# Delta rule: the part that needs the roots of keys and queries, issued three projection steps later

## The chip, the core and the metric

The kernel runs on one core of a Trainium2 chip. The metric is the device time of one execution in microseconds. The engines are TensorE (PE in the rows; PEld is its weight load), VectorE (DVE), ScalarE (ACT), GpSimd (POOL) and SyncE (SP), which issues the DMAs here.

## The reference

A two-layer decoder trunk on a sequence of 2048 rows of 1024: a gated DeltaNet layer, then a forgetting-attention layer. Only the first is touched. Cut to what matters:

```python
qkv = silu(causal_depthwise_conv(qkv, conv_w))      # 4 taps
q, k, v = split(qkv, 3)
q, k = l2_norm(q), l2_norm(k)                       # per head, 128 channels, 8 heads
...
a_mat = where(strict, einsum('cd,sd->cs', k * beta, k) * decay, 0)
attn  = einsum('cd,sd->cs', q, k) * decay
u, w  = triangular_solve(I + a_mat, [v * beta, k * beta * exp(gcum)])
...                                                 # per chunk: state S from u, w, k, attn
```

The root is that of `l2_norm`: `rsqrt(sum(x*x) + eps)` for each row of q and k.

## The kernel before

The first stage walks over four blocks of 512 rows (q0 to q3) and in each over four pairs of heads, so over 16 pairs. For one pair `project` issues eight projections in the order K, Q, V of the first head, K, Q, V of the second, then the gates z of both. A projection is eight steps (`kt` 0 to 7) of three 128x128x512 matmuls (L130 to L132), with a `yield` after each step. Weights come through SP (L312, L313) for blocks after the first; in q0 they are split on ScalarE and POOL on the way (L320, L322).

Behind each of K, Q and V stands a `tail`: ScalarE makes two copies of the product (L386, L390), VectorE adds the three other taps of the convolution (L387, three L392), ScalarE takes a tanh (L395), and VectorE makes the SiLU of it (L400), into `kq` for keys and queries. `tail` returns a `rest`, which goes into the list `pend`; it is taken out at step 6 of a later projection, when more than one stands there. So the `rest` of Q runs at step 6 of the projection after next: of the second head's K for the first head, of the first gate z for the second. It transposes on TensorE (L407), takes squares on ScalarE (L411), adds eps on VectorE (L417), and POOL takes the power -0.5 (`rsqrt`, L119). Then come what needs the root: four small instructions on VectorE (L419 to L424, which give `rq`, `brk2` and `vs`), and per two chunks the products of keys with keys and queries on TensorE (L430) and three wide instructions on VectorE (L434 twice, L437), which write `At` and `attn`.

Beside the projections of one pair runs `finish` of the pair before, a generator that `weave` advances after every step. It reads `At`: four DMAs out (L469), four back in another shape (L472), a substitution of 62 dependent VectorE instructions (L478, L480), DMAs back (L483, L485), then transposes into `Tn` (L488). After 45 steps it goes on with the solver's products on TensorE (L494, into X1 by L498 and L499, then L505), and after these with the recurrence over the chunks (L540 to L577), whose results are scaled (L595) and written out (L599, L601).

A scheduler places the instructions of each engine in a list before the run: among those that it expects to be ready, the one that comes first in the program goes first, and one from further down may fill a hole. Each engine then works through its list in order. Tiles come from pools with a few buffers each; the product tile `pk` and the decay's `pdf` share two PSUM buffers.

Of the kernel before, what the change touches and what calls it, by code (L numbers as in the profile page):

```python
# [9 lines left out]
F32 = mybir.dt.float32  # L10
# [4 lines left out]
ALU = mybir.AluOpType  # L15
# [3 lines left out]
P = 128  # L19
# [5 lines left out]
SCALE = P ** -0.5  # L25
# [103 lines left out]
def mm3(nc, out, ah, al, bh, bl, start, stop):  # L129
    nc.tensor.matmul(out, ah, bh, start=start, stop=False)  # L130
    nc.tensor.matmul(out, ah, bl, start=False, stop=False)  # L131
    nc.tensor.matmul(out, al, bh, start=False, stop=stop)  # L132


def gdn(k, ins, oT_d, chain, proj_, after_proj):

    nc, tc = k.nc, k.tc
    NQ, TB, CH = 4, 512, 4
# [12 lines left out]
    pq = pool(proj_, "gpq", 2, "right", space=PSUM)  # L151
# [143 lines left out]
    def project(qt, hg, state, tiles):  # L295
        xh, xl = state[:2]
        q_ = f"q{qt}"
        gn = f"{q_}g{hg}"
        kqs, vRs, kds, late = [], [], [], []
        At = c2.tile([P, U, P], F32, tag="At", name=f"At_{gn}")  # L300
        attn = c2.tile([P, U, P], F32, tag="attn", name=f"attn_{gn}")
        zT = c2.tile([P, G, TB], F32, tag="zT", name=f"zT_{gn}")
        rq = c2.tile([P, U], F32, tag="rq", name=f"rq_{gn}")
# [24 lines left out]
        def proj(col, nm):  # L328
            wh, wl = wsplit(col, nm)
            pp = pm.tile([P, TB], F32, tag="mm", name=f"pp_{nm}")  # L330
            if turns:
                turns.pop(0)()
            for kt in range(KT):
                if len(turns) > 1:
                    turns.pop(0)()
                mm3(nc, pp, wh[:, kt, :], wl[:, kt, :], xh[kt], xl[kt], kt == 0, kt == KT - 1)
                if kt == 6 and len(pend) > 1:
                    pend.pop(0)()
                yield
            if turns:  # L340
                turns.pop(0)()
            return pp
# [15 lines left out]
        for hl in range(G):  # L358
            h = hg * G + hl
            us = slice(hl * CH, (hl + 1) * CH)  # L360
            kq = c2.tile([P, CH, 2, P], F32, tag="kq", bufs=4, name=f"kq_{q_}_{h}")
            vR = c2.tile([P, CH, P], F32, tag="vR", bufs=4, name=f"vR_{q_}_{h}")
            kd = c2.tile([P, CH, P], F32, tag="kd", bufs=4, name=f"kd_{q_}_{h}")
            kqs.append(kq)
            vRs.append(vR)
            kds.append(kd)
            E = p2.tile([P, CH, P], F32, tag="E", name=f"E_{q_}_{h}")
            if len(state) > 2:
                decays(h, E)
            else:  # L370
                late.append(lambda: decays(0, E))
            ssn = p2.tile([P, 2, CH], F32, tag="ssn", name=f"ssn_{q_}_{h}")
            rn = p2.tile([P, 2, CH], F32, tag="rn", name=f"rn_{q_}_{h}")
            vs = p2.tile([P, CH], F32, tag="vs", name=f"vs_{q_}_{h}")
            for kind in (1, 0, 2):
                ct = kind * H + h
                nm = f"{q_}_{ct}"
                pp = yield from proj(ct * P, nm)
                if len(late) > 0:
                    late.pop(0)()  # L380
                beta, eg = state[2], state[5]

                def tail(h=h, hl=hl, us=us, kq=kq, vR=vR, kd=kd, E=E, ssn=ssn, rn=rn, vs=vs, kind=kind, ct=ct, nm=nm, pp=pp):
                    cx = p2.tile([P, TB + 3], F32, tag="cx", name=f"cx_{nm}")
                    nc.vector.tensor_copy(cx[:, 0:3], halo[:, ct, :])
                    nc.scalar.copy(cx[:, 3:], pp)  # L386
                    nc.vector.tensor_copy(halo[:, ct, :], cx[:, TB:TB + 3])  # L387
                    cw = [k.cols[:, C_CONV + j * 24 + ct:C_CONV + j * 24 + ct + 1] for j in range(4)]
                    acc = p2.tile([P, TB], F32, tag="acc", name=f"acc_{nm}")
                    nc.scalar.activation(acc, pp, AF.Copy, scale=cw[3])  # L390
                    for j in range(3):
                        nc.vector.scalar_tensor_tensor(out=acc, in0=cx[:, j:j + TB], scalar=cw[j], in1=acc,  # L392
                                                       op0=ALU.mult, op1=ALU.add)
                    th = p2.tile([P, TB], F32, tag="th", bufs=3, name=f"th_{nm}")
                    nc.scalar.activation(th, acc, AF.Tanh, scale=0.5)  # L395
                    if kind == 2:
                        src = th.rearrange("p (c t) -> p c t", t=P)
                    else:
                        src = kq[:, :, 1 - kind, :]
                    nc.vector.scalar_tensor_tensor(out=src, in0=th.rearrange("p (c t) -> p c t", t=P), scalar=1.0,  # L400
                                                   in1=acc.rearrange("p (c t) -> p c t", t=P),
                                                   op0=ALU.add, op1=ALU.mult)

                    def rest():
                        pt = pm.tile([P, CH, P], F32, tag="tr", name=f"pt_{nm}")
                        for c in range(CH):
                            nc.tensor.transpose(out=pt[:, c, :], in_=src[:, c, :], identity=k.ident)  # L407
                        if kind < 2:
                            for c in range(CH):
                                junk = p2.tile([P, P], BF16, tag="junk2", name=f"j_{nm}_{c}")  # L410
                                nc.scalar.activation(junk, pt[:, c, :], AF.Square, accum_out=ssn[:, kind, c:c + 1])  # L411
                        if kind == 1:
                            for c in range(CH):
                                nc.scalar.activation(kd[:, c, :], pt[:, c, :], AF.Copy,
                                                     scale=eg[:, 2, c, h:h + 1])
                        if kind == 0:
                            nc.vector.tensor_scalar(out=ssn, in0=ssn, scalar1=4.0 * EPS, scalar2=None, op0=ALU.add)  # L417
                            rsqrt(k, rn.rearrange("p a b -> p (a b)"), ssn.rearrange("p a b -> p (a b)"), 2 * CH)
                            nc.vector.tensor_scalar(out=rq[:, us], in0=rn[:, 0], scalar1=SCALE, scalar2=None,  # L419
                                                    op0=ALU.mult)  # L420
                            nc.vector.tensor_tensor(out=brk2[:, us], in0=rn[:, 1], in1=rn[:, 1], op=ALU.mult)
                            nc.vector.tensor_tensor(out=brk2[:, us], in0=brk2[:, us], in1=beta[:, :, h],
                                                    op=ALU.mult)
                            nc.vector.scalar_tensor_tensor(out=vs, in0=ssn[:, 1], scalar=0.5, in1=rn[:, 1],  # L424
                                                           op0=ALU.mult, op1=ALU.mult)
                            for cc in range(0, CH, 2):
                                pk = pq.tile([P, 2, 2, P], F32, tag="kkq", name=f"pk_{q_}_{h}_{cc}")
                                for c in (cc, cc + 1):
                                    u = hl * CH + c
                                    nc.tensor.matmul(pk[:, c - cc].rearrange("p a b -> p (a b)"), kq[:, c, 0, :],  # L430
                                                     kq[:, c].rearrange("p a b -> p (a b)"), start=True, stop=True)
                                for c in (cc, cc + 1):
                                    u = hl * CH + c
                                    nc.vector.scalar_tensor_tensor(out=At[:, u, :], in0=pk[:, c - cc, 0, :],  # L434
                                                                   scalar=brk2[:, u:u + 1], in1=E[:, c, :],
                                                                   op0=ALU.mult, op1=ALU.mult)
                                nc.vector.tensor_tensor(out=attn[:, hl * CH + cc:hl * CH + cc + 2, :], in0=pk[:, :, 1, :],  # L437
                                                        in1=E[:, cc:cc + 2, :], op=ALU.mult)
                        if kind == 2:
                            for c in range(CH):  # L440
                                nc.scalar.activation(vR[:, c, :], pt[:, c, :], AF.Copy, scale=vs[:, c:c + 1])

                    return rest

                pend.append(tail())


        for hl in range(G):
            h = hg * G + hl
# [150 lines left out]
                                           in1=zT[:, hl, :], op0=ALU.mult, op1=ALU.mult)  # L600
            nc.sync.dma_start(oT_d[h, :, t0:t0 + TB], og)  # L601

    pend = []
    state = prep(0)
    sides = []
    for qt in range(NQ):
# [704 lines left out]
```

## Time and profile before

| | us |
|---|---|
| median of three runs | 2905.1 (2903.18 to 2905.47) |
| profiled execution | 2906.06 |
| its span | 2904.3 |
| TensorE busy | 2797.7 (96%) |
| VectorE busy | 1715.9 (59%) |
| ScalarE busy | 1335.7 (46%) |
| POOL busy | 704.6 (24%) |

Busy time is the time in which the engine had an instruction in work; ends of matmuls are modelled. Times in rows are counted from the start of the span. In a row of the timeline the first number is the start, the second the time that the instructions of the row took together, `x4` their count, and the bracket the engine's idle time just before and who ended it.

### The profile page before, as it was taken

To read this page: it belongs to the slowest core of one execution; us is meant where nothing else is said; L and a number is where in the kernel's file an instruction comes from. 1 tells how busy PE (TensorE), PEld (TensorE's weight loads), DVE (VectorE), ACT (ScalarE), POOL (GpSimd) and SP (SyncE) were. 2 spreads that over 40 slices of the span, in tenths; PEclk is the share of its full clock that TensorE was granted. 3 is DMA by queue.
4 is the path that set the end of the run, shared out by engine and by line. 5 is a ranking of instruction groups with operands and counts; after the bars stand their busy time and mean duration, and the time that the engine had idled before them with its cause. 6 is when DMAs were issued, how large, how long until landed. Compare 5 with 4: busy or idle time off the path is not lost.

```text
span 2904.3 us, 50700 instructions
## 1 busy us (share of the span) xinstructions
PE 2797.7 (96%) x18406; PEld 2434.2 (84%) x18406; DVE 1715.9 (59%) x5060; ACT 1335.7 (46%) x3695; POOL 704.6 (24%) x712
## 2 busy tenths in 40 slices
PE   7889999999999999899999999999999999999998
PEld 6677788878887788787999999999998888888787
DVE  6776777777777777635333124332329888888422
ACT  5445544454444444434344223443227677676421
POOL 6544211121111111122211000110004444443322
PEclk9999999999999999999999999999999999999999
DMA  7656444444443443636322323223323323332443
GB/s 234 215 163 191 148 153 137 159 151 130 151 158 118 154 137 108 190 116 200 95 88 88 96 95 113 95 88 94 112 82 101 98 91 98 93 96 76 158 140 109
DMA packets 295505, 371.64 MB, mean 128 GB/s; under 512 B 68443, under 2 KB 216150, under 8 KB 294230
## 3 DMA queue, kind: packets, MB, share of 16 engines
q1 hardware_dynamic: 295088, 368.33, 40.0%
q8 instruction: 145, 2.38, 0.4%
q14 instruction: 106, 0.87, 0.1%
q10 hardware_dynamic: 166, 0.06, 0.0%
HBM read 263.40 MB, written 104.92 MB: 127 GB/s over the span
## 4 chain that ended last, share of the span: by engine, by line
PE 66%; DVE 17%; ACT 3%; issue 3%; POOL 2%; DMA 1%; DVEq 0%; POOLq 0%; SPq 0%; ACTq 0%
DVE acc_q L392 4%; PE pt L1134 4%; PE ppv L130 2%; PE ps L132 2%; PE ppq L130 2%; PE ppv L131 2%; PE ppv L132 2%; PE ppq L131 2%; PE ppq L132 2%; PE ppwf L130 2%; PE ppwf L131 2%; PE ppwf L132 2%; PE ppz L130 2%; PE ppz L131 2%; PE ppz L132 2%
## 5 line engine op out<-in xcount | busy, mean ns | idle before, releaser
L130 PE MATMUL pp_q<-xh_q,wh_q 128*128 128x512 f32 x768 | 325.4, 424 | 1.5 <-ACT acc_q L390 0.8
L132 PE MATMUL pp_q<-xh_q,wl_q 128*128 128x512 f32 x768 | 307.2, 400 | 0.0
L131 PE MATMUL pp_q<-xl_q,wh_q 128*128 128x512 f32 x768 | 305.4, 398 | 0.0
L392 DVE SCALAR_TENSOR_TENSOR acc_q<-cx_q,cols,acc_q 128x512 f32<-128x512 f32 x288 | 227.1, 789 | 13.0 <-ACT acc_q L390 9.7
L125 DVE TENSOR_TENSOR pl<-pt,ph 128x512 fp32r<-128x512 f32 (+1 forms) x320 | 191.8, 605 | 37.9 <-ACT ph L124 36.0
L124 ACT CAST ph<-pt 128x512 fp32r<-128x512 f32 (+1 forms) x320 | 161.8, 519 | 90.5 <-PE pt L1134 89.7
L395 ACT ACTIVATE th_q<-acc_q 128x512 f32<-128x512 f32 x96 | 60.6, 632 | 277.1 <-DVE acc_q L392 273.7
L1120 ACT ACTIVATE s<-s,nm 128x128 f32<-128x128 f32 (+15 forms) x128 | 154.3, 1206 | 67.2 <-DVE nm L1118 67.0
L1134 PE MATMUL pt<-ident,s 128*128 128x128 f32 x1088 | 172.1, 273 | 3.3 <-DVE pl L125 2.4
L132 PEld LDWEIGHTS pp_q<-xh_q,wl_q 128*128 128x128 f32 x768 | 145.5, 189 | 33.9
L130 PEld LDWEIGHTS pp_q<-xh_q,wh_q 128*128 128x128 f32 x768 | 146.1, 190 | 27.4 <-ACT acc_q L390 1.3
L131 PEld LDWEIGHTS pp_q<-xl_q,wh_q 128*128 128x128 f32 x768 | 146.0, 190 | 26.4 <-DVE xl_q L240 0.8
L1134 PEld LDWEIGHTS pt<-ident,s 128*128 128x128 f32 x1088 | 133.5, 140 | 33.4 <-DVE pl L125 3.6
L130 PE MATMUL ppk<-wh_k,hh 128*128 128x256 f32 x512 | 147.7, 288 | 2.6 <-issue 2.6
L130 PE MATMUL ppq<-wh_q,hh 128*128 128x256 f32 x512 | 146.8, 287 | 0.0
L130 PE MATMUL ppv<-wh_v,hh 128*128 128x256 f32 (+1 forms) x512 | 144.9, 283 | 0.0
L131 PE MATMUL ppk<-wl_k,hh 128*128 128x256 f32 x512 | 144.6, 282 | 0.0
L132 PE MATMUL ppk<-wh_k,hl 128*128 128x256 f32 x512 | 144.4, 282 | 0.0
L130 PE MATMUL ppz<-wh_z,hh 128*128 128x256 f32 x512 | 144.3, 282 | 0.0
L132 PE MATMUL ppv<-wh_v,hl 128*128 128x256 f32 (+1 forms) x512 | 143.9, 281 | 0.0
L131 PE MATMUL ppv<-wl_v,hh 128*128 128x256 f32 (+1 forms) x512 | 143.9, 281 | 0.0
L132 PE MATMUL ppq<-wh_q,hl 128*128 128x256 f32 x512 | 143.7, 281 | 0.0
(482 smaller groups left out, 8568.2 us busy)
## 6 DMA issues: line engine op xcount, KB each, us to landing
wh_q<-w_d SPq DMA_DIRECT2D x72, 512.0 KB, 3.6
wl_q<-w_d SPq DMA_DIRECT2D x72, 512.0 KB, 4.9
w_d<-wh_q SPq DMA_DIRECT2D x24, 512.0 KB, 4.8
w_d<-wl_q SPq DMA_DIRECT2D x24, 512.0 KB, 3.1
wh_q_z<-w_d SPq DMA_DIRECT2D x24, 512.0 KB, 3.4
wl_q_z<-w_d SPq DMA_DIRECT2D x24, 512.0 KB, 4.3
wr_q<-in_gdn_w_in_dram SPq DMA_DIRECT2D x22, 512.0 KB, 5.7
x_q<-in_x_dram SPq DMA_DIRECT2D x16, 512.0 KB, 4.8
```

Of the source, the lines that this page charges most:

```text
L124: i = k.nc.scalar.copy(hi, src)
L125: (eng or k.nc.vector).tensor_tensor(out=lo, in0=src, in1=f(hi), op=ALU.subtract)
L130: nc.tensor.matmul(out, ah, bh, start=start, stop=False)
L131: nc.tensor.matmul(out, ah, bl, start=False, stop=False)
L132: nc.tensor.matmul(out, al, bh, start=False, stop=stop)
L392: nc.vector.scalar_tensor_tensor(out=acc, in0=cx[:, j:j + TB], scalar=cw[j], in1=acc, op0=ALU.mult, op1=ALU.add)
L395: nc.scalar.activation(th, acc, AF.Tanh, scale=0.5)
L1120: e = nc.scalar.activation(s[:, 0:w], s[:, 0:w], AF.Exp, bias=nm, accum_out=ls[:, ii:ii + 1])
L1134: nc.tensor.transpose(out=pt[:, ii * P:(ii + 1) * P], in_=Ps[ii][:, j * P:(j + 1) * P], identity=k.ident)
```

## The change

The part of `rest` that needs the root becomes a function `products`, which `rest` of a Q returns. The step that calls `rest` puts it into a list `soon`, and step 1 of the next projection calls it: steps 7, 0 and 1 lie between. For the first head of a pair that is step 1 of the second head's Q, for the second head step 1 of the second gate.

```diff
                 mm3(nc, pp, wh[:, kt, :], wl[:, kt, :], xh[kt], xl[kt], kt == 0, kt == KT - 1)
+                if kt == 1 and soon:
+                    soon.pop(0)()
                 if kt == 6 and len(pend) > 1:
-                    pend.pop(0)()
+                    more = pend.pop(0)()
+                    if more:
+                        soon.append(more)
                 yield
...
+                    def products():
+
+                        nc.vector.tensor_scalar(out=rq[:, us], in0=rn[:, 0], scalar1=SCALE, scalar2=None,
+                                                op0=ALU.mult)
...
+                        for cc in range(0, CH, 2):
+                            pk = pq.tile([P, 2, 2, P], F32, tag="kkq", name=f"pk_{q_}_{h}_{cc}")
...
+                            nc.vector.tensor_tensor(out=attn[:, hl * CH + cc:hl * CH + cc + 2, :], in0=pk[:, :, 1, :],
+                                                    in1=E[:, cc:cc + 2, :], op=ALU.mult)
+
                     def rest():
...
                         if kind == 0:
                             nc.vector.tensor_scalar(out=ssn, in0=ssn, scalar1=4.0 * EPS, scalar2=None, op0=ALU.add)
                             rsqrt(k, rn.rearrange("p a b -> p (a b)"), ssn.rearrange("p a b -> p (a b)"), 2 * CH)
...
+                            return products
...
-    pend = []
+    pend, soon = [], []
```

The body of `products` is what stood in `rest`, word for word.

## Rows read from the trace of the kernel before

**Rows 1.** Busy time by stretch: PE, PEld, DVE, ACT, POOL; clock, DMA share, GB/s

```profile
410.00:480.00 70.00, 68.44 (x448) 56.58 (x448) 51.09 (x177) 31.90 (x109) 10.66 (x9) 1.00 0.47 148
```

**Rows 2.** TensorE's waits, 340 to 1165 us: total us, times, longest

```profile
PE py_q1g L505 <- ACT X_q1g L498: 3.2, 4, 1.1
...
PE py_q1g L505 <- DVE X_q1g L499: 0.9, 4, 0.2
...
PE px_q1g L494 <- DVE Tn L488: 0.8, 2, 0.4
```

**Rows 3.** TensorE's waits, 100 to 340 us

```profile
PE px_q0g L494 <- DVE Tn L488: 11.8, 6, 2.7
PE pt_q L407 <- DVE kq_q L400: 9.8, 5, 4.3
```

**Rows 4.** Timeline of VectorE, first head of a pair in q1

```profile
431.22 0.17 DVE L417 TENSOR_SCALAR ssn_q<-ssn_q 128x8 f32<-128x8 f32 x1
433.14 0.17 DVE L419 TENSOR_SCALAR rq_q1g<-rn_q 128x4 f32<-128x4 f32 x1 [1.75 <-POOL rn_q L119]
...
435.39 0.16 DVE L387 COPY halo<-cx_q 128x3 f32<-128x3 f32 x1
...
436.12 0.29 DVE L474 COPY Ti_q1g<-unit 128x256 f32<-128x256 f32 x1
...
438.55 0.69 DVE L400 SCALAR_TENSOR_TENSOR kq_q<-th_q,acc_q 128x512 f32<-128x512 f32 x1 [0.50 <-ACT th_q L395]
...
439.82 0.89 DVE L488 STREAM_TRANSPOSE Tn<-At_q1g 32x256 f32<-32x256 f32 x2
```

**Rows 5.** Timeline of ScalarE in the same pair

```profile
429.10 0.69 ACT L390 ACTIVATE acc_q<-pp_q,cols 128x512 f32<-128x512 f32 x1
437.89 0.63 ACT L395 ACTIVATE th_q<-acc_q 128x512 f32<-128x512 f32 x1 [8.09 <-DVE acc_q L392]
...
444.31 0.63 ACT L395 ACTIVATE th_q<-acc_q 128x512 f32<-128x512 f32 x1 [3.69 <-DVE acc_q L392]
...
447.03 0.36 ACT L498 COPY X_q1g<-px_q1g 32x256 f32<-32x256 f32 x1
```

**Rows 6.** Line L419: what ended VectorE's idle time before it, us, times

```profile
  POOL rn_q L119: 55.6, 32
```

**Rows 7.** Timeline of TensorE, second head of the same pair

```profile
450.47 1.89 PE L430 MATMUL pk_q<-kq_q 128*128 128x256 f32 x8
...
454.39 1.14 PE L518 MATMUL px_q1g<-Tn,At_q1g 64*64 64x64 f32 x16
```

**Rows 8.** Timeline of SP there, and line L472's time to landing

```profile
459.70 1.71 SPq L472 DMA_DIRECT2D Ai_q1g<-d_q1g  x4
...
DMA to landing us min/median/max: 2.8/3.8/7.1
```

**Rows 9.** Timeline of VectorE there: the substitution begins

```profile
467.47 0.35 DVE L573 SCALAR_TENSOR_TENSOR S<-S,eg_q,pa_q1g 128x128 f32<-128x128 f32 x1 [3.97 <-PE pa_q1g L567]
...
468.39 0.18 DVE L478 TENSOR_TENSOR tmp_q1g<-Ti_q1g,Ai_q1g 128x31 f32<-128x31 f32 x1
```

**Rows 10.** Timeline of POOL and VectorE at a root in q0

```profile
201.63 1.64 POOL L119 TENSOR_TENSOR rn_q<-ssn_q,mhalf 128x8 f32<-128x8 f32 x1 [2.22 <-DVE ssn_q L417]
201.71 0.18 DVE L480 TENSOR_TENSOR Ti_q0g<-Ti_q0g,tmp_q0g 128x8 f32<-128x8 f32 x1
203.31 0.69 DVE L419 TENSOR_SCALAR rq_q0g<-rn_q 128x4 f32<-128x4 f32 x1 [1.42 <-POOL rn_q L119]
```

**Rows 11.** Another root, of x's rows, beside VectorE; line L119's min/median/max ns

```profile
298.39 0.75 DVE L392 SCALAR_TENSOR_TENSOR acc_q<-cx_q,cols,acc_q 128x512 f32<-128x512 f32 x1
298.51 1.49 POOL L119 TENSOR_TENSOR xrs_q<-xss_q,mhalf 128x4 f32<-128x4 f32 x1 [15.07 <-DVE xss_q L225]
...
L119 POOL TENSOR_TENSOR xrs_q<-xss_q,mhalf x7: 549/1007/1494, 6.0 to 624.5; 128x1 f32<-128x1 f32 x4, 128x4 f32<-128x4 f32 x3
```

**Rows 12.** Timeline of SP: the solver's last DMAs before L488

```profile
431.26 1.89 SPq L485 DMA_DIRECT2D At_q1g<-d_q1g  x4
```

More of the change, by code (lines that the diff above doesn't have):

```diff
@@ L402, in tail @@
                                                    op0=ALU.add, op1=ALU.mult)
+                    def products():
+                        nc.vector.tensor_scalar(out=rq[:, us], in0=rn[:, 0], scalar1=SCALE, scalar2=None,
+                                                op0=ALU.mult)
+                        nc.vector.tensor_tensor(out=brk2[:, us], in0=rn[:, 1], in1=rn[:, 1], op=ALU.mult)
+                        nc.vector.tensor_tensor(out=brk2[:, us], in0=brk2[:, us], in1=beta[:, :, h],
+                                                op=ALU.mult)
+                        nc.vector.scalar_tensor_tensor(out=vs, in0=ssn[:, 1], scalar=0.5, in1=rn[:, 1],
+                                                       op0=ALU.mult, op1=ALU.mult)
+                        for cc in range(0, CH, 2):
+                            pk = pq.tile([P, 2, 2, P], F32, tag="kkq", name=f"pk_{q_}_{h}_{cc}")
+                            for c in (cc, cc + 1):
+                                u = hl * CH + c
+                                nc.tensor.matmul(pk[:, c - cc].rearrange("p a b -> p (a b)"), kq[:, c, 0, :],
+                                                 kq[:, c].rearrange("p a b -> p (a b)"), start=True, stop=True)
+                            for c in (cc, cc + 1):
+                                u = hl * CH + c
+                                nc.vector.scalar_tensor_tensor(out=At[:, u, :], in0=pk[:, c - cc, 0, :],
+                                                               scalar=brk2[:, u:u + 1], in1=E[:, c, :],
+                                                               op0=ALU.mult, op1=ALU.mult)
+                            nc.vector.tensor_tensor(out=attn[:, hl * CH + cc:hl * CH + cc + 2, :], in0=pk[:, :, 1, :],
+                                                    in1=E[:, cc:cc + 2, :], op=ALU.mult)
                     def rest():
@@ L418, in rest @@
                             rsqrt(k, rn.rearrange("p a b -> p (a b)"), ssn.rearrange("p a b -> p (a b)"), 2 * CH)
[L419 to L438, printed above, removed]
+                            return products
                         if kind == 2:
```

## Prediction

> **What bounds the kernel now.** Only the delta-rule stage is touched, the first 1165 us of the span. I read it in four steps. First, busy time by stretch: in 70 us of the steady part TensorE is busy for 68.4 us, VectorE for 51.1 and ScalarE for 31.9 [rows 1]. TensorE sets the pace, so VectorE time counts only where TensorE waits for it. Second, what TensorE waited for from 340 to 1165 us: above all two products of the solver, L494 for Tn (VectorE, L488) and L505 for X1 (ScalarE L498, then VectorE L499). The rows for block q1 are 3.2 us (ScalarE X1), 0.9 (VectorE X1) and 0.8 (Tn) [rows 2]; with eight like rows of the other blocks they come to 7.4, 2.5 and 2.9 us, 12.8 us over twelve pairs of heads. Eight of these pairs wait for more than 1 us in all (one in q0, three in q1, two each in q2 and q3), four for about 0.4. From 100 to 340 us, where three more pairs lie, it is 11.8 us for Tn and 9.8 us for kq [rows 3]. So some 34 us is all that a quicker VectorE could return here.
>
> Third, why Tn and X1 are late: the VectorE list of one pair [rows 4]. L417 of the first head runs at 431.22; then VectorE idles 1.75 us for POOL's root, runs the four small readers and the six wide products (433.14 to 435.39), and only then begins the convolution of the pair's second K projection, which has been waiting. Its tanh leaves 0.50 us more in which VectorE idles before L400. Three L488 follow from 439.82, and then the next convolution. Fourth, the ScalarE list: it idles 8.09 us before the first of these two tanh and 3.69 us before the second, both times for VectorE, and X1 comes 2.7 us after the second one [rows 5]. So the chain to TensorE's wait is VectorE's list from 431 to 444 us. Each us of idleness in it costs TensorE a us, up to the wait of that pair.
>
> The stall before L419 is there 32 times, 55.6 us in all [rows 6], but half of it is free: in the second head's half of a pair VectorE stands idle later anyway, 3.97 us ahead of the first state update [rows 9].
>
> **The change, part by part.** No instruction is added or removed; 14 per head (four small VectorE readers, four PE products that run as eight passes, six wide VectorE products) are issued three steps later, for 32 heads. No DMA moves in the program; what moves is the order.
>
> *PE.* The eight passes take 1.89 us, and three steps 2.0 us (452.36, the end of the passes, to 454.39) [rows 7]. They change places, which is zero on TensorE. For the second head the passes now end at about 454.4, and the root arrives no earlier; so its products end where they did, or up to 0.7 us later if the gate product L455 slips ahead of them. For the first head VectorE is so far behind that ScalarE's copies of the second K, ready at 429.8, wait until 435.39 [rows 4, 5]; the passes will be done when it wants them. The last step of the second K ends 1.9 us earlier, and ScalarE's two copies of it with it; they already wait for VectorE.
>
> *The wide products, first head.* With the readers they last 2.25 us [rows 4]. Behind the convolution they no longer delay its tanh, and they can fill the 0.50 us before L400 and the smaller holes of that stretch (about 0.1 us ahead of the first L434, some 0.035 us between dependent L392), 0.84 us together. Bounds: 0 and 0.84 us per pair. I take the upper one, since the trace shows holes of this list filled with whatever is ready: L474, a copy for a solver that starts over 40 steps later in the program, stands behind the first L392 [rows 4]. Eight pairs give 6.7 us; four are capped at their 0.4 us, 1.6; three in block q0 give 2.4. Sum 10.7 us; I take 10, as not every hole will be met.
>
> *The stall itself.* Does the convolution come between L417 and L419? By the program, yes. But the list is laid out by when results are thought to be there, and it counts the root short: at 201 us L480, 0.18 us long, is the last to stand between the two, and then the engine waits for 1.42 us more [rows 10]; in steady pairs nothing stands there. The readers need only the root. The convolution needs ScalarE's two copies, which stand behind the squares that L417 itself waited for. So I expect the readers right behind L417 as now. Bounds: 0 and 1.75 us saved per first head; I take 0.
>
> If one L392 does come between, little is won: at 298 us a root issued 0.12 us after the start of an L392 took 1.49 us, against a median of 1.01 [rows 11], as if it began when that L392 ended. One L392 then hides nothing, three hide the root.
>
> On this the Trainium skill, "SBUF — State Buffer", section "Who interferes with whom", has a stronger rule: a VectorE instruction with two SBUF inputs and a GpSimd instruction that reads SBUF exclude each other for the whole instruction, whichever is first. The case at 298 us agrees with it. The L480 at 201.71, which has two SBUF inputs and took 0.18 us inside a root that had begun at 201.63, does not [rows 10]. By the rule a root that is first would hold the convolution up for its 1.64 us, and the change could give no more than my forecast even with the order that the program asks for.
>
> *Later in the pair.* The second head's At is ready up to 0.7 us later; SP waits for it at L469, and behind that stands L472. L472's first issue at 459.70 lands after a median of 3.8 us, and the substitution begins at 468.39 [rows 8, 9]: 5 us of cover for 0.7.
>
> **Rivals.**
> *The stall goes too.* The convolution's three L392 run while POOL takes the root. VectorE then gains 1.75 + 0.84 us, more than any steady pair waits: all 12.8 us go, and in block q0 three pairs times 2.4 us, 7.2. That is 20 us, so 2885; with the restart of the pipeline after each wait it may be 25. For it: in the run itself the copies that the convolution reads are there at 429.8, before L417 [rows 5]. Against: rows 10, and that the order is made before the run.
>
> *It does not do what it says.* VectorE works in order, and the work between L417 and the second tanh is the same; if the readers keep their place and the holes stay, the chain is as long as before: 2905, give or take 2. For it: all the work of that stretch stays in it. Against: the products now stand right behind the 0.50 us hole.
>
> *Slower: the solver's substitution is laid out later.* As the list expects it, the second head's products come some 2 us later, and so L469, L472 and the first L478. Its 62 dependent instructions end in DMAs, the last of which (L485) leaves at 433.15 [rows 12]; with 3.8 us for the landing, as in rows 8, L488 at 439.82 has 2.9 us to spare. Up to that point nothing is lost. If the substitution slips by a whole convolution of 2.3 us on top of the 2 us, L488 waits 1.4 us, VectorE with it, and L494 has no cover: 15 pairs times 1.4 us less what the holes give back, some 10 to 20 us: 2918. Against: the 5 us of cover at its start.
>
> **How the numbers follow.** The profiled execution took 2906.06 us (the span of 2904.3 and 1.8 around it), 1.0 above the median of 2905.1; 10 us of it are 10 us of the median. Forecast 2895, own range 2891 to 2900, chance 0.46. Stall gone, 2885 (2879 to 2889): 0.20. Nothing, 2903 to 2907: 0.22. Slower, 2911 to 2925: 0.12. The range for 8 in 10 runs from 2880 to 2908. What a measurement can tell from no change is about 0.2%, 5.8 us. Faster than that: 0.85 of the forecast's 0.46 and all of the 0.20, 0.59. Slower: 0.12. Within: 0.29.
>
> **What would show it.** After the change L419 to L424 still stand right behind L417 with 1.6 to 1.8 us of idleness, then L387 and three L392, then L434 and L437 around L400; no idle time before L400; the wait of L494 near zero and that of L505 smaller. If the idle time at L419 is far below 55.6 us in all, the first rival is right; if L400 still idles 0.5 us and L505 waits as before, the second; if L488 idles for a DMA, the third. I would be wrong in kind if the order changed in places far from these heads.

## The result and the profile after

The changed kernel takes 2922.41 us (median of six runs, 2919.51 to 2928.41) beside 2904.25 us for the kernel before in the same comparison (2902.00 to 2905.47): ratio 1.0067, 95% interval 1.0054 to 1.0080. It is slower, by some 18 us; forecast were 2895 us and a range of 2880 to 2908. Its profiled execution has a span of 2921.3 us against 2904.3, 17.0 more.

Lines of the changed kernel, with those of before in brackets: substitution L486 and L488 (L478, L480), Tn L496 (L488), px L502 (L494), py L513 (L505), readers of the root from L410 (L419), convolution L396 (L392), SP's L477, L480, L491, L493 (L469, L472, L483, L485). In kernels that delay one head alone, lines from L448 on have numbers two higher still (Tn L498, px L504).

**TensorE's waits.** From 340 to 1185 us, as [rows 2] (total us, times, longest):

```profile
PE px_q1g L502 <- DVE Tn L496: 6.9, 6, 1.6
PE px_q2g L502 <- DVE Tn L496: 6.6, 6, 1.6
PE px_q3g L502 <- DVE Tn L496: 6.3, 6, 1.7
```

The waits for X1 are all but gone (0.4 us; before 10.0 by the same view; in *first* below, where px does not wait from 340 us on, 4.2 are left). In their place stand 19.8 us for Tn, which were 2.9.

**Idle and busy.** Busy time by stretch, columns as [rows 1]: from the first projection product of the second pair of q1 to the last one of q3 (called "q1 to q3" below); before, then after.

```profile
394.60:1165.30 770.70, 754.26 (x4898) 619.20 (x4897) 562.88 (x1912) 357.38 (x1187) 118.39 (x98) 1.00 0.44 140
```
```profile
391.70:1177.80 786.10, 761.61 (x4899) 622.54 (x4898) 555.11 (x1912) 354.27 (x1188) 120.69 (x98) 0.98 0.42 137
```

This stretch is 15.4 us longer; what lies ahead of it is 2.9 us shorter, what lies behind it 4.5 us longer, which makes the 17.0. Only 8.1 us of the 15.4 is idleness (16.4 to 24.5); 7.4 us is busy time, for the same matmuls. The granted clock says why. Two waits of px in the changed kernel, and what follows them:

```profile
439.51 0.22 PE L502 MATMUL px_q1g<-Tn,At_q1g 32*32 32x32 f32 x2 [1.59 <-DVE Tn L496]
...
799.85 0.22 PE L502 MATMUL px_q2g<-Tn,At_q2g 32*32 32x32 f32 x2 [1.59 <-DVE Tn L496]
```
```profile
440.00:442.00 2.00, 1.18 (x32) 0.80 (x30) 1.84 (x4) 1.55 (x9) 0.00 (x0) 0.85 0.89 262
442.00:444.00 2.00, 2.00 (x9) 1.55 (x6) 0.60 (x2) 1.47 (x3) 0.00 (x0) 0.50 0.89 308
444.00:446.00 2.00, 2.00 (x9) 1.59 (x8) 1.82 (x3) 0.07 (x1) 0.00 (x0) 0.79 0.80 263
...
802.00:804.00 2.00, 2.00 (x22) 1.64 (x15) 0.97 (x4) 1.54 (x3) 0.00 (x0) 1.00 0.95 275
```

Each pair waits twice, for the first and for the last part of Tn: 1.59 and 0.82 us in the first, 1.59 and 0.81 in the second. Behind the first pair's wait the clock is at 0.50 (1.2 instead of 2.4 GHz), and the projection products start 0.43 us apart. Behind the second pair's it stays at 1.00, and they start 0.23 us apart. (The counts of the rows, x9 and x22, also hold small products of px.) The first of these pairs takes 70.47 us, the second 68.97: 1.5 us for one fall. In windows of 1 us over q1 to q3, the time below full clock is worth 11.9 us of full clock (before: 3.4).

**Why Tn is late.** VectorE in the pair of [rows 4], columns as there; before, then after:

```profile
427.09 0.17 DVE L480 TENSOR_TENSOR Ti_q1g<-Ti_q1g,tmp_q1g 128x8 f32<-128x8 f32 x1
...
429.37 0.17 DVE L581 TENSOR_TENSOR s_q1g<-rq_q1g 128x8 f32<-128x8 f32 x1 [1.75 <-POOL s_q0g L119]
```
```profile
426.60 0.17 DVE L589 TENSOR_TENSOR s_q1g<-rq_q1g 128x8 f32<-128x8 f32 x1 [1.62 <-POOL s_q0g L119]
...
426.76 0.18 DVE L486 TENSOR_TENSOR tmp_q1g<-Ti_q1g,Ai_q1g 128x24 f32<-128x24 f32 x1
426.88 1.66 DVE L603 TENSOR_SCALAR vR_q<-vR_q,s_q0g 128x128 f32<-128x128 f32 x8
...
428.77 0.77 DVE L396 SCALAR_TENSOR_TENSOR acc_q<-cx_q,cols,acc_q 128x512 f32<-128x512 f32 x1
...
430.47 0.17 DVE L410 TENSOR_SCALAR rq_q1g<-rn_q 128x4 f32<-128x4 f32 x1 [0.84 <-POOL rn_q L119]
...
432.02 0.17 DVE L488 TENSOR_TENSOR Ti_q1g<-Ti_q1g,tmp_q1g 128x8 f32<-128x8 f32 x1
...
436.23 0.29 DVE L482 COPY Ti_q1g<-unit 128x256 f32<-128x256 f32 x1 [0.81 <-DMA d_q1g<-Ti_q1g]
...
436.51 2.32 DVE L396 SCALAR_TENSOR_TENSOR acc_q<-cx_q,cols,acc_q 128x512 f32<-128x512 f32 x3
...
438.94 0.42 DVE L496 STREAM_TRANSPOSE Tn<-At_q1g 32x256 f32<-32x256 f32 x1
...
440.25 0.90 DVE L496 STREAM_TRANSPOSE Tn<-At_q1g 32x256 f32<-32x256 f32 x2
```

Before, the substitution is over when VectorE begins to wait for the root of the output's scaling (L581). After, its last six instructions stand behind that wait and among eight scalings, a wait for the first head's root (0.84 us) and a convolution: they run from 426.76 to 432.19 us, for 1.1 us of work. From the first projection product of the pair (394.6 and 391.7 us) the substitution ends after 32.6 us before and 40.5 now, the last Tn after 46.8 and 49.5.

The time between the substitution's end and Tn is used up as well. SP's last DMAs in this pair, and line L493's time to landing:

```profile
436.19 1.81 SPq L493 DMA_DIRECT2D At_q1g<-d_q1g  x4
```
```profile
DMA to landing us min/median/max: 1.8/2.4/3.9
```

By the median the four land between some 438.6 and 440.4 us. The last two L496 begin at 440.25, so that little could have been won by an earlier place for them in the list; before, by the prediction's reckoning, the landing was 2.9 us ahead of L488 [rows 4, 12].

It also starts later. SP and VectorE a pair on, as [rows 8, 9], and line L480's time to landing:

```profile
455.85 1.80 SPq L477 DMA_DIRECT2D d_q1g<-At_q1g  x4
460.75 0.34 SPq L312 DMA_DIRECT2D wh_q<-w_d  x1
461.31 1.70 SPq L480 DMA_DIRECT2D Ai_q1g<-d_q1g  x4
```
```profile
DMA to landing us min/median/max: 3.5/4.0/5.9
```
```profile
469.73 0.35 DVE L556 SCALAR_TENSOR_TENSOR R_q1g<-pa_q1g,neg_q,vR_q 128x128 f32<-128x128 f32 x1 [1.92 <-PE pa_q1g L549]
...
470.49 0.75 DVE L396 SCALAR_TENSOR_TENSOR acc_q<-cx_q,cols,acc_q 128x512 f32<-128x512 f32 x1
471.16 0.18 DVE L486 TENSOR_TENSOR tmp_q1g<-Ti_q1g,Ai_q1g 128x31 f32<-128x31 f32 x1
```

Against the next pair's first product (462.8 before, 462.2 after), L477 leaves as early as L469 did (6.3 us ahead, before 6.2); a weight load now stands ahead of L480 (0.8 us ahead, before 3.1). By the median, Ai lands at some 465.3, and L486 runs 5.9 us later, 9.0 us into the pair, where L478 came after 5.6. Between the two VectorE stands idle for 1.92 us, until TensorE has the product that L556 needs, and then begins the next convolution; ahead of L486 the profile shows no idle time. Its place in VectorE's list holds it, not its data.

### The profile page after: what moved, and what is told of

It reads as the page before. It is cut to its first block, busy times and chain, and to the rows that moved or that the text cites. A ratio compares the mean times of both kernels' runs of the same rounds, so it can differ in the third digit from the quotient of the medians.

```text
span 2921.3 us, 50695 instructions
## 1 busy us (share of the span) xinstructions
PE 2805.0 (96%) x18406; PEld 2436.4 (83%) x18406; DVE 1713.6 (59%) x5060; ACT 1330.5 (46%) x3695; POOL 706.3 (24%) x712
## 4 chain that ended last, share of the span: by engine, by line
PE 69%; DVE 17%; DMA 4%; ACT 3%; POOL 3%; issue 3%; SPq 1%; DVEq 0%; POOLq 0%; ACTq 0%
DVE acc_q L396 4%; PE pt L1142 4%; PE pp_q_z L130 2%; PE ppv L130 2%; PE ppq L130 2%; PE ppv L131 2%; PE ppv L132 2%; PE ppq L131 2%; PE ppq L132 2%; PE ps L132 2%; PE ppz L130 2%; PE ppwf L132 2%; PE ppwf L130 2%; PE ppz L132 2%; PE ppwf L131 2%
## 5 line engine op out<-in xcount | busy, mean ns | idle before, releaser
L396 DVE SCALAR_TENSOR_TENSOR acc_q<-cx_q,cols,acc_q 128x512 f32<-128x512 f32 x288 | 229.2, 796 | 10.5 <-ACT acc_q L394 8.0
L131 PE MATMUL ppq<-wl_q,hh 128*128 128x256 f32 x512 | 143.7, 281 | 0.0
```

## Experiments

Ratios are to the kernel before, run beside. "Tn": TensorE's wait for it, 340 to 1185 us. "Pair": mean of the second and third pair of q1, q2 and q3, from first projection product to first projection product. "Clock": what the time below full clock in q1 to q3 is worth. All in us.

| kernel | median | ratio (95%) | Tn | pair | clock |
|---|---|---|---|---|---|
| before | 2904 to 2908 | 1 | 2.9 | 68.5 | 3.4 |
| the change | 2922.4 | 1.0067 (1.0054 to 1.0080) | 19.8 | 70.4 | 11.9 |
| first | 2894.8 | 0.9962 (0.9950 to 0.9974) | 0 | 67.0 | 0 |
| second | 2941.8 | 1.0131 (1.0116 to 1.0145) | 29.9 | 72.3 | 20.5 |
| first_hop | 2952.1 | 1.0156 (1.0140 to 1.0172) | 30.2 | 72.6 | 25.6 |
| after_prev | 2886.1 | 0.9931 (0.9918 to 0.9943) | 0 | 66.6 | 0 |
| dose2 | 2898.3 | 0.9978 (0.9968 to 0.9988) | 0 | 67.1 | 0 |
| first_z4 | 2950.2 | 1.0156 (1.0141 to 1.0172) | 0 (px2: 28.9) | 71.4 | 25.6 |
| after_short24 | 2879.7 | 0.9912 (0.9898 to 0.9925) | 0 | 66.3 | 0 |
| first_short24 | 2872.7 | 0.9884 (0.9869 to 0.9900) | 0 | 66.0 | 0 |
| after_46 | 2924.3 | 1.0066 (1.0053 to 1.0079) | 20.0 | 70.7 | 11.9 |
| after_47 | 2918.9 | 1.0046 (1.0030 to 1.0061) | 13.5 | 68.6 | 3.4 |
| after_Ti2 | 2929.3 | 1.0077 (1.0061 to 1.0094) | 19.6 | 71.4 | 20.5 |
| first_46 | 2892.7 | 0.9958 (0.9946 to 0.9971) | 0 | 67.0 | 0 |
| after_fill | 2932.5 | 1.0086 (1.0073 to 1.0100) | 4.5 | 69.5 | 0 |
| second_fill | 2947.1 | 1.0135 (1.0120 to 1.0151) | 2.2 | 71.2 | 0 |
| first_fill | 2919.2 | 1.0039 (1.0027 to 1.0052) | 0 | 68.8 | 0 |

### Which head costs

```diff
-                            return products
+                            if hl == 0:
+                                return products
+                            products()
```

*first* (this one; in *second* the test is `hl == 1`):

> Only the first head of each pair issues its products three steps later; the second head issues them at once, as before the change. Theory (the second head's delay lays the solver's substitution out later, and that makes Tn late): the substitution starts and ends where it did before, TensorE's wait of px for Tn falls from the changed kernel's 19.8 us (340 to 1185 us) back to under 4, and the first head's gain that was forecast is left: 2892 to 2898 us. Rival (the first head's own delay is at fault, since it lets convolutions in between the last substitution steps): px waits 15 us or more and the time is 2912 to 2925.

> Only the second head of each pair issues its products three steps later; the first head issues them at once. Theory: the substitution starts some 3 us later in its pair than before the change, Tn comes later by that, TensorE waits for Tn, and nothing is gained at X1: 2908 to 2922 us. If the slack of 2.9 us before Tn takes up the shift, since no convolution lies between the last substitution steps here, 2904 to 2908. Rival (the first head's delay is at fault): substitution and waits as before the change, 2902 to 2906.

The first head alone gives 2894.8 us and no wait for Tn; VectorE there, in the pair of [rows 4]:

```profile
434.37 0.17 DVE L444 TENSOR_SCALAR ssn_q<-ssn_q 128x8 f32<-128x8 f32 x1
434.44 0.17 DVE L391 COPY halo<-cx_q 128x3 f32<-128x3 f32 x1
436.28 0.17 DVE L410 TENSOR_SCALAR rq_q1g<-rn_q 128x4 f32<-128x4 f32 x1 [1.68 <-POOL rn_q L119]
...
436.43 0.75 DVE L396 SCALAR_TENSOR_TENSOR acc_q<-cx_q,cols,acc_q 128x512 f32<-128x512 f32 x1
...
437.91 0.35 DVE L425 SCALAR_TENSOR_TENSOR At_q1g<-pk_q,brk_q1g,E_q 128x128 f32<-128x128 f32 x1
438.17 0.75 DVE L396 SCALAR_TENSOR_TENSOR acc_q<-cx_q,cols,acc_q 128x512 f32<-128x512 f32 x1
...
439.67 0.69 DVE L404 SCALAR_TENSOR_TENSOR kq_q<-th_q,acc_q 128x512 f32<-128x512 f32 x1
```

The stall stays, the convolution and the wide products share what follows, and L404 runs without a wait, where L400 had one of 0.50 us. The second head alone is worse than the whole change. There the substitution's last steps stand behind both roots with their full 1.62 us, and Tn behind products and two convolutions; the first Tn even waits for its DMA:

```profile
428.73 0.17 DVE L591 TENSOR_TENSOR s_q1g<-rq_q1g 128x8 f32<-128x8 f32 x1 [1.62 <-POOL s_q0g L119]
...
432.60 0.17 DVE L410 TENSOR_SCALAR rq_q1g<-rn_q 128x4 f32<-128x4 f32 x1 [1.62 <-POOL rn_q L119]
...
443.09 0.43 DVE L498 STREAM_TRANSPOSE Tn<-At_q1g 32x256 f32<-32x256 f32 x1 [0.42 <-DMA At_q1g<-d_q1g]
```

So the first head's part brings 11 us and the second head's loses 27.6 us on top of it (2922.4 less 2894.8; the two medians come from different comparisons, and by the ratios it is some 30). The size for the second head alone, some 36 us, was underestimated by the theory, which had 2922 us, some 17 more than before, as its most.

### The products, or the substitution's start

*first_hop* delays the substitution's input alone; *after_prev* does the opposite and frees the substitution from the late products.

```diff
+        d0 = pd.tile([4, U, 32, 32], F32, tag="d0", name=f"d0_{gn}")
+        nc.sync.dma_start(d0.rearrange("b u s c -> (b u) (s c)"), d1.rearrange("b u s c -> (b u) (s c)"))
         for cg in range(NG):
-            nc.sync.dma_start(Ai[cg * NB:(cg + 1) * NB], d1.rearrange("b u s c -> (b u) s c"))
+            nc.sync.dma_start(Ai[cg * NB:(cg + 1) * NB], d0.rearrange("b u s c -> (b u) s c"))
```

> Only the first head's products are late, as in the run that took 2894.8 us; the second head's come at once. Added is one more copy in DRAM between the blocks of At that SP writes out and the load of Ai, so that the substitution's input alone is known later. The extra hop is not on TensorE. Theory (what costs the time is that the substitution is laid out later, whatever makes it late): the substitution starts some 3 us or more later in its pair and ends 5 us or more later, px waits 15 us or more for Tn from 340 to 1185 us, 2912 to 2940 us. Rival (the second head's late products cost the time in themselves, by PE's passes, the kq and pk tiles or VectorE's wide products): 2892 to 2900.

In *after_prev* the same load reads the `d1` of the pair before, kept in a list (`d1` has a third buffer for it, which is not shown):

```diff
+        olds.append(d1)
+        dp = olds[max(0, len(olds) - 2)]
         for cg in range(NG):
-            nc.sync.dma_start(Ai[cg * NB:(cg + 1) * NB], d1.rearrange("b u s c -> (b u) s c"))
+            nc.sync.dma_start(Ai[cg * NB:(cg + 1) * NB], dp.rearrange("b u s c -> (b u) s c"))
```

> The whole change, both heads late, but each substitution loads its input Ai from the blocks that the pair before wrote out, so that it does not depend on the second head's late products (the solve is of the wrong pair; work and transfers stay the same). Theory (the second head's lateness costs only through the substitution's start): the substitution starts as early as before the change or earlier, px waits under 4 us for Tn from 340 to 1185 us, 2884 to 2898 us. Rival (the late products of the second head cost in themselves): 2910 to 2922.

| second head's products | substitution's input with them | otherwise |
|---|---|---|
| at once | 2894.8 | one hop later: 2952.1 |
| three steps late | 2922.4 | from the pair before: 2886.1 |

The time follows the substitution, not the products: with the hop the loss is there though the products are on time (12 us above the 2940 expected, which was not taken apart; the time below full clock, 25.6 us beside 11.9 in the whole change, is of that size), and with late products and early input it is gone. In the six pairs of the column "Pair", the substitution starts 5.6 us into the pair in *first* and before the change, 9.0 in the whole change and in *second*, 10.9 in *first_hop* and 5.4 in *after_prev*; it ends after 32.6, 40.5 (*second*: 39.5), 41.6 and 30.7 us.

### How much delay

*dose2* delays the first head by three steps and the second by two; *first_z4* keeps the first head's delay and moves the second head the other way.

```diff
-                if kt == 1 and soon:
-                    soon.pop(0)()
+                if soon and kt == (1, 0)[soon[0][0]]:
+                    soon.pop(0)[1]()
...
-                            return products
+                            return hl, products
```

> First head's products three steps late, second head's two steps instead of three. Theory (the loss comes by the substitution's place in VectorE's list, which moves in jumps): at two steps it still starts ahead of the first convolution of its pair, so it ends within 2 us of where it did before, and most of the loss is gone: 2893 to 2903 us. Rival (each step of delay of the second head costs its share of the 27 us between the run with the first head alone and the whole change): two thirds of them, 2909 to 2916.

```diff
-                if kt == 6 and len(pend) > 1:
+                if kt == (4 if '_z' in nm else 6) and len(pend) > 1:
```

> The kernel with the first head alone late, and in addition the step at which the second head's Q (and V) is transposed and squared is moved ahead, from step 6 of the gates' projections to step 4: its products come two steps earlier than before the change. Theory (an earlier start of the substitution is worth time wherever px still waits for Tn): in block q0 and for the last pair px waits 13.9 and 2.4 us with the first head alone; some 5 to 12 of these go, 2882 to 2891 us. Rival (the earlier transposes wait for the second head's kq, which VectorE has not made yet): new waits of pt for kq of 5 us or more, 2893 to 2905.

Two steps cost 3.5 us over none and three cost 27.6, so the loss comes as a jump, not by the step. The trace shows the jump: at two steps the substitution starts 5.6 us into its pair in the six pairs, exactly as with none, at three after 9.0. The 3.5 us are not in the steady pairs (67.1 beside 67.0); the profiled executions of the two part behind the last projection product, beside the last pair's solver.

*first_z4* came out far above both of its cases. What both expected is there: px's waits in q0 fall from 14.9 to 6.9 us, and those of pt for VectorE's L404 rise from 6.5 to 12.2. But both are small beside a product further on, px2 (L528), which waits for its Tn 28.9 us (340 to 1185 us):

```profile
469.66 1.61 PE L528 MATMUL px_q1g<-Tn,At_q1g 64*64 64x64 f32 x13 [3.23 <-DVE Tn L521]
```
```profile
465.79 0.17 DVE L410 TENSOR_SCALAR rq_q1g<-rn_q 128x4 f32<-128x4 f32 x1 [1.75 <-POOL rn_q L119]
...
469.10 0.42 DVE L521 TENSOR_SCALAR Tn<-py_q1g 32x256 f32<-32x256 f32 x1
```

L521 now stands behind the second head's root and products. It looks like the fault of the change at another part of the solver: something with a root in it was put ahead of what TensorE needs next. No run tested that.

### The end of the substitution

```diff
-        for j in range(31):
+        for j in range(24):
```

> The changed kernel with the last 7 of the 31 steps of the substitution left out (14 of 62 VectorE instructions, about 0.2 us each, so the solve is incomplete). Those are the ones that stand among and behind the output scaling's root and the first head's root in the changed kernel. Theory (px waits because the substitution ends behind these two roots): it ends some 6 us earlier, px waits under 4 us for Tn, and the time falls to 2888 to 2902. Rival (Tn's place on VectorE behind the convolution, or the second head's products, are at fault, not the end of the substitution): px still waits 12 us or more, 2912 to 2922.

> The control for the run before: the same last 7 steps of the substitution left out, with the first head's products late and the second head's at once. The 2.8 us of VectorE work per pair that are gone stand where TensorE did not wait for Tn. Theory: 2888 to 2896, little under the 2894.8 of the same kernel with all 31 steps, and within 5 us of the run before. Rival (fewer instructions help as such, 14 x 0.2 us a pair): 2850 to 2880.

Both came out below what the theory expected, the control in its rival's range. The cut brings 22.1 us to the kernel without the fault, so fewer steps do help as such: in q0, where px waited 13.9 us with the first head alone (6.3 with the cut), and 1 us a pair later. But it brings 42.7 us to the whole change, and the distance between the two falls from 27.6 to 7.0 us. Some 20.6 us of the loss go with the steps that stand behind the roots; the other 22.1 come to the control as well and say nothing on the change. In *after_short24* the substitution still starts 9.0 us into its pair, but ends after 30.3 us, and px does not wait from 340 us on: the late start costs nothing where the end is early enough. The 7.0 us that are left stand in the profiled executions for the most part behind the last projection product (it ends at 1137.6 and 1136.4 us), as with *dose2*.

### Where px and Tn stand

*after_46* and *after_47* move px one and two steps later in the program and leave py where it was.

```diff
-W_INV, W_PY, W_PX2, W_PY2, W_A, W_B, W_C, W_OUT, W_OUT2 = 45, 5, 4, 2, 2, 1, 2, 9, 1
+W_INV, W_PY, W_PX2, W_PY2, W_A, W_B, W_C, W_OUT, W_OUT2 = 46, 4, 4, 2, 2, 1, 2, 9, 1
```

> The changed kernel with px one step later (46 steps instead of 45 behind the start of finish, and 4 instead of 5 from px to py, so that everything from py on stays at its step). One step is 1.07 us of TensorE's work. Theory (the loss is px standing ahead of Tn on TensorE): of some 1.5 us that px waits in each steady pair one step hides 1.07, so about 10 to 13 us come back, 2907 to 2913, and px waits 6 to 10 us instead of 19.8. Rival (the time is lost in VectorE's longer list, wherever px stands): 2919 to 2925.

> The changed kernel with px two steps later (47 instead of 45, and 3 instead of 5 from px to py). Theory: 2.1 us of cover are more than px waits, so that its wait falls under 4 us; py had about 4 us to spare and loses 2.1 of them: 2899 to 2906 us. Rival (the wait only moves to the next one that reads X1, or the time is lost in VectorE's list): px waits little, py waits 10 us or more, 2915 to 2925.

One step changes nothing: px begins sooner on the first part of Tn and then waits longer for the second (0.90 and 1.44 us in a pair that had 1.59 and 0.81). That is the rival's range. With two the pair is down to 68.6 and the clock falls but twice; yet px still waits 13.5 us (under 4 were expected), and the median gives back only 3.5 us. In the profiled execution, at 2922.9 us one of the slower of six, the second pair of q0 took 80.1 us (72.2 in the changed kernel). That was not followed up, and by the total the expectation failed.

*after_Ti2* gives Ti a second buffer.

```diff
-        Ti = c1.tile([P, NS, 32], F32, tag="Ti", name=f"Ti_{gn}")
+        Ti = c1.tile([P, NS, 32], F32, tag="Ti", bufs=2, name=f"Ti_{gn}")
```

> The whole change with a second buffer for Ti. In the changed kernel the copy that starts the next solver waits some 0.8 us in each steady pair until SP's transfer has read Ti (7.7 us in blocks q1 to q3), and the convolution and Tn stand behind it on VectorE. If VectorE's own order is what makes Tn late: 6 to 8 us come back, 2913 to 2917. If the landing of the solver's blocks is what holds Tn, the wait only moves to Tn: 2919 to 2924.

This one is inconclusive, since it did not take the wait away. With a second buffer every copy (L482) is laid out one pair earlier, the first one of q1 at 285.0 us instead of 368.4. What stands at 436.65 us is the copy for the solver after next, and it waits 0.81 us for the same transfer. Tn and its waits are as in the changed kernel; the time below full clock is worth 20.5 us instead of 11.9, and the median is 6.9 us higher. Whether that wait matters stays untested.

### The clock

*after_fill* puts 12 products of the identity ahead of px, *second_fill* 20, *first_fill* 12 where nothing waits.

```diff
+        for i in range(12):
+            nc.tensor.matmul(px[:, 0:4, :].rearrange("p u c -> p (u c)"), k.ident, k.ident, start=True, stop=True)
```

> The whole change with 12 extra 128x128 products of the identity with itself on TensorE right ahead of px in each of the 16 pairs (about 0.15 to 0.2 us each by the rows of the transposes, 1.8 to 2.4 us a pair; their results are overwritten). They only add work. In the changed kernel the granted clock of TensorE falls to 0.50 behind most of the waits of px; summed over blocks q1 to q3 the time at half clock is worth 11.9 us, against 3.4 before the change. Theory (the clock that falls behind the wait is a cost of its own): the products run where TensorE stood idle, the clock stays at 1.00, and 12 to 15 us come back less 4 to 8 us in the pairs that did not wait: 2911 to 2918 us. Rival (idle time is all that is lost): no gain, 2921 to 2935.

> The kernel with the second head alone late, with 20 such products ahead of px in each pair (3 to 4 us). There px waits up to 3.6 us for Tn and time at half clock is worth 20.5 us in q1 to q3. Theory (clock): most of the 20.5 us come back less some 9 to 12 us in the pairs that wait less than the products last: 2928 to 2936 us. Rival (idle time alone): 2941 to 2960.

> The control: 12 such products ahead of px in the kernel with the first head alone late, in which px waits for nothing in q1 to q3 and the clock stays at 1.00 there. Both theories: the products cost their own time in 12 or 13 pairs, 1.8 to 2.4 us each less the 0.6 us for which py waits, and nothing in q0: 2909 to 2925 us.

By the totals the theory's numbers failed, and both kernels fall into their rival's range: the whole change goes from 1.0067 to 1.0086 with the added work, the second head alone from 1.0131 to 1.0135, which is no gain. Beside the control (0.9962 to 1.0039, 22 us) that is little, and the pairs tell why. In the control a pair takes 1.8 us longer (67.0 to 68.8), which is the price of the 12 products. In the whole change it takes 0.9 us less (70.4 to 69.5), in *second_fill*, whose products cost about 3 us, 1.1 less (72.3 to 71.2), and in both the clock stays at 1.00 throughout q1 to q3; for the whole change:

```profile
399.80:1186.50 786.70, 777.96 (x5163) 645.30 (x5162) 556.04 (x1912) 354.78 (x1188) 120.01 (x98) 1.00 0.43 137
```

If idleness were all that is lost, work put into it could at best leave the pair as it was. It got shorter, so the clock is a cost of its own, about 1 us a pair net. Nor did the added work move the solver: in *after_fill* the substitution starts and ends and the last Tn comes 9.0, 40.5 and 49.5 us into the pair, as in the whole change. But the stretch as a whole is no shorter (786.7 us, 786.1 without the products): in pairs that had not waited, and behind the last projections, the products only cost. The Trainium skill, "TensorE: Matmul & The Clock Gate", section "HAM oscillation — how this bites in real kernels", tells of products that start at the lower clock again and again because each was waited for. The rows at 442 us agree; those at 802 us, behind a wait as long, do not.

### The best version

*first_46* is *first* with the 46 and 4 of *after_46*.

> The kernel with the first head alone late, px one step later and py where it was (46 and 4 in place of 45 and 5). In its blocks q1 to q3 TensorE no longer waits at px and some 0.6 us a pair at py; in q0 px waits 13.9 us. If px's place costs anything there: up to one step in each of the three pairs of q0 and in the last one, 2889 to 2893 us. If py, not px, is what is late now: no change, 2892 to 2897.

It lies where its two cases overlap: 2892.7 us, ratio 0.9958, not told apart from *first* (0.9962). Both beat the kernel before by about 0.4% and the change by 1%.

## Why the prediction was wrong

- **The reading of the bound held.** TensorE sets the pace, and what it waits for are X1 and Tn [rows 2]. That a us of waiting costs a us was too little: 8.1 us more idleness came with 7.4 us more busy time in q1 to q3.
- **TensorE's passes at zero: right.** In *first* and in *after_prev* they stand three steps later and nothing is lost.
- **The first head's products in holes: right in the steady pairs, and the total partly luck.** In *first* the 0.50 us ahead of L400 are gone, the last Tn comes 1.2 us earlier in its pair (46.8 to 45.6), and the pair shrinks by 1.2 us beside its usual 68.2 (0.84 forecast). The kernel gains some 11 (10 forecast), but otherwise than by the sum: in the profiled executions q1 to q3 give 14 us, 3.4 of them time below full clock that is gone, and what lies ahead, from which 2.4 us were to come (three times 0.84 would be 2.5), loses 3.2.
- **The stall stays: right where the substitution keeps its place.** In *first* L410 still idles 53.0 us in all (55.6 before, [rows 6]). In the whole change it is 47.2, since one L396 came in between.
- **"One L392 hides nothing": wrong in seven cases of twelve.** See the last section.
- **The failed step: "5 us of cover for 0.7".** The second head's At leaves when forecast, and Ai still lands some 6 us ahead of the first instruction of the substitution. But in [rows 8, 9] the gap between landing (463.5) and start (468.39) was taken for cover, and so for the sign that a later input costs nothing. It is the list's order: with its input later, the substitution was laid behind the next convolution's start, and its tail behind two waits for roots. Its start slipped 3.4 us within the pair, its end 7.8, which used up the slack ahead of Tn; TensorE's wait for Tn rose from 2.9 to 19.8 us. That the start slipped by the list and not by the landing is shown by the idle time ahead of L556 and by the jump between two steps and three; what the scheduler expected, and for when, stands in no trace.
- **The slower rival was the right one, at a chance of 0.12.** 2918 us (2911 to 2925), measured 2922.4. It had the place right and three sizes off: the end slipped 7.8 us, not 4.3; L496 hardly waits for DMAs (0.7 us in all from 390 to 1165 us, and 3.5 for the last pair), it stands behind VectorE's other work, shortly after its data land; and the clock was not in it. It was given little for the 5 us at the start, while its own price lay at the end, where the slack was 2.9 us [rows 4, 12].

## What to carry to other kernels

When a list is made before the run, a wait of an instruction for its own place looks like cover in the profile: ask whether its engine idles ahead of it for the data, and if it does not, take the gap for order, which a small delay can make jump. Price a delay where the chain ends, not where it begins, and keep dependent chains ahead of, not among, instructions that wait for another engine. Move one part at a time: here half of the change is worth 0.4%, and the other half costs more than twice that.

## What the runs showed of the hardware

A wait can cost TensorE more than its length. Of the nine pairs of q1 to q3 in the changed kernel that waited for Tn, for 1.7 to 2.4 us, six were followed by a stretch at half clock, worth 1.7 us of full clock and once 3.4 (1.5 us between the two pairs shown above), and three by none.

A root on POOL beside an L396 on VectorE depends on hundredths of a microsecond. Timeline of POOL in two pairs of the changed kernel:

```profile
428.80 1.64 POOL L119 TENSOR_TENSOR rn_q<-ssn_q,mhalf 128x8 f32<-128x8 f32 x1 [2.23 <-DVE halo L391]
```
```profile
568.52 2.16 POOL L119 TENSOR_TENSOR rn_q<-ssn_q,mhalf 128x8 f32<-128x8 f32 x1 [2.29 <-DVE tmp_q1g L486]
```

The first root began 0.02 us after an L396 and took its usual 1.64 us, while that L396 took 0.77 us instead of 0.75; seven of the 32 are like it. The second began 0.08 us after an L396 and took 0.52 us longer, as if held; four, 0.08 to 0.10 us behind, are like that, and a fifth, 0.03 us behind, took 2.22. So one L396 can hide 0.9 us of a root, against what was read from [rows 11]. The Trainium skill, "SBUF — State Buffer", section "Who interferes with whom", has the later of the two blocked for the whole of the other's instruction. The second case agrees but for 0.14 us: the L396 had 0.66 us left when the root began. The first does not: there VectorE ran an L396 and an L488, both with two SBUF inputs, inside a root.
